# Order of partial products, casts and stores in a hybrid attention, RWKV-7 and feed-forward block

## The chip, the core and the metric

One NeuronCore of a Trainium2 chip runs the whole block. The number is the device time of one execution in microseconds (us). The engines are named as the profile names them: PE (TensorE, matmuls; PEld is its weight loads), DVE (VectorE), ACT (ScalarE), POOL (GpSimd), SP (SyncE, which only issues transfers). Each engine takes its instructions in order from a queue of its own, and waits at the head of the queue for what the next instruction needs.

## The reference

x has 2048 tokens of 1024 channels, all in float32. Cut to what matters here:

```
h  = rms_norm(x, pre_mix_g)
P  = h @ w_in                                   # q, k, v, RWKV inputs, gates
yA = chunk_band_attention(q, k, v, rel_bias)    # 8 heads of 64
yB = rwkv7_time_mix(...)                        # 8 heads of 64
m  = sigmoid(gA) * (yA @ proj_a) + sigmoid(gB) * (yB @ proj_b)   # "branches"
x  = x + rms_norm(m @ w_out, post_mix_g)                         # "output projection"
x  = x + rms_norm(relu(rms_norm(x, pre_ffn_g) @ w_up)**2 @ w_down, post_ffn_g)   # FFN, 4096 wide
```

## The kernel before

Every float32 operand of a matmul is split into a high and a low part (names ending in h and l, or hi and lo): `split` lets ScalarE cast the tile (L78) and VectorE subtract the cast from it (L79). A product is then three matmuls, high by high, low by high, high by low, added in one PSUM bank; a matmul has 512 columns.

The tokens go in four groups of 512 (`G`), one after the other through `phase_rwkv`, `phase_attention` and `phase_merge`; then the FFN runs in two halves of 1024 tokens, each `phase_up` and `phase_down`. In the FFN both weight matrices are cut into 2 by 2 blocks, and seven block products replace eight; the sums of blocks pass through DRAM (xd, wd, td).

**Branches.** `phase_attention` computes the heads in pairs. At its end, while the last pair is still being computed, `load_y` loads and splits the RWKV result (yraw, yh, yl), and `branch` multiplies it by proj_b for eight blocks of 128 channels into ps_p, two banks in turn. A block takes four k tiles with three matmuls each, which `mm3` issues k by k. `phase_merge` then does the same with proj_a. VectorE multiplies each bank by the gate th, which is loaded, at L1097.

**Output projection.** `phase_merge` then multiplies the merged m (mh, ml) by w_out, in two halves of 512 columns (n = 0, 1), weights loaded and split in pairs of k (whi, wlo). Four banks ps_o hold the four tiles of 128 tokens. For each k and each token tile three matmuls are issued in a row. When a half is done, ScalarE squares each bank (sqo, L1136) and VectorE multiplies it by the gain (o, L1137), which frees it. In between come steps of the next group's first norm (`between`: squares L349, scale xn L351, eight transposes pstr L147, casts hh L152 and hl L153) and sums of blocks for the FFN (`beside`, cmb). The next group's first matmul is psd<-hh,whi.

**FFN up.** In tile i of `phase_up` the casts are a1h and a1l of the first weight tile (from i = early = 8 on), s12h, s4h and s3h of block sums; X holds the seven block values that go to DRAM.

**FFN down.** `phase_down` does the block products "1", "6", "7", "5", "4", "3", "2", each in eight steps f. A step loads and splits an activation and a weight tile into one tile fop, two steps ahead. `final(t)` closes an output tile of 128 tokens: square (squ, L1427), gain (L1428), root on POOL (rs), scale and add (L1434), store. The tiles GT + t are complete after product "4", the tiles t after "2"; `advance` runs one step of such a generator. `first_half(2)` loads and splits the next half's activations (bl, bh).

A scheduler orders each engine's queue by the program's order, the buffers that come free and its own estimate of durations; `queue_behind(a, b)` puts a behind b in an engine's order without a wait.

Of the kernel before, what the change touches and what calls it, by code (L numbers as in the profile page):

```python
# [9 lines left out]
F32 = mybir.dt.float32  # L10
# [43 lines left out]
class Block:  # L54
# [1031 lines left out]
    def branch(self, y, br, i):  # L1086

        nc, mp = self.nc, self.bp
        t = mp.tile([P, G], F32, tag="th", bufs=3, name="th")
        nc.sync.dma_start(t, self.gd[br * KB + i])  # L1090
        if i % 2 == 0:
            w = self.a[("proj_a", "proj_b")[br]][:, i * P : (i + 2) * P]
            self.bw = self.wsplit(w.rearrange("(k p) n -> p k n", p=P), "w", NP, 2 * P)
        wh, wl = (x[:, :, i % 2 * P : (i % 2 + 1) * P] for x in self.bw)
        ps = self.pd.tile([P, G], F32, tag="d", name="ps_p")
        self.mm3(ps, [(wh[:, k], wl[:, k], y[0][:, k], y[1][:, k]) for k in range(NP)])
        nc.vector.scalar_tensor_tensor(t, t, 1.0, ps, op0=ALU.add, op1=ALU.mult)  # L1097
        return t

    def phase_merge(self, g, o, op, between, beside):  # L1100

        tc, nc, a = self.tc, self.nc, self.a
        with ExitStack() as ctx:
# [13 lines left out]
            for n in range(2):  # L1117
                ps = [po.tile([P, 512], F32, tag="o", name="ps_o") for _ in range(GT)]
                for k in range(KB):
                    if k % 2 == 0:  # L1120
                        w = a["w_out"][k * P : (k + 2) * P, n * 512 : (n + 1) * 512]
                        wh, wl = self.wsplit(w.rearrange("(j p) n -> p j n", p=P), "w", 2, 512)
                    for t in range(GT):
                        ts = slice(t * P, (t + 1) * P)
                        for j, (l, r) in enumerate(((mh, wh), (mh, wl), (ml, wh))):
                            nc.tensor.matmul(  # L1126
                                ps[t], l[:, k, ts], r[:, k % 2], start=k == 0 and j == 0, stop=k == KB - 1 and j == 2
                            )
                    if n == 0 and k in ((2, 4, 5, 6, 7) if g + 1 < self.NG else (0, 2, 3, 4, 5)):
                        advance(beside, 1)  # L1130
                    if n == 0 and k == 4 or n == 1 and k % 2 == 0:
                        advance(between, 1)
                ns = slice(n * 512, (n + 1) * 512)
                for t in range(GT):
                    sq = op.tile([P, 512], F32, tag="sqo", bufs=2, name="sqo")
                    nc.scalar.activation(sq, ps[t], AF.Square, accum_out=self.ssq[:, g, t, n : n + 1])  # L1136
                    nc.vector.tensor_tensor(o[t][:, ns], ps[t], gp[:, ns], ALU.mult)  # L1137
# [73 lines left out]

    def split_here(self, hi, lo):

        self.nc.scalar.copy(hi, lo.bitcast(F32))
        self.nc.vector.tensor_tensor(lo, lo.bitcast(F32), hi.bitcast(F32), ALU.subtract)

    def first_half(self, g, bp):

        bh, bl = self.b1 = [bp.tile([P, KB, G], F32R, tag="b" + x, name="b" + x) for x in "hl"]
        for k in range(0, KB, 2):  # L1220
            ks = slice(k, k + 2)
            self.nc.sync.dma_start(bl[:, ks].bitcast(F32), self.ht[g][:, ks])
            self.split_here(bh[:, ks], bl[:, ks])
            yield

    def phase_up(self, half, zp, rp, cb, pn, early):
# [6 lines left out]
        with ExitStack() as ctx:  # L1233
# [36 lines left out]
            def parts(src, tag, n):  # L1270
                pool = sp if tag in ("a1", "s12") else late
                hl = [pool.tile([P, n, P], F32R, tag=tag + x, name=tag + x) for x in "hl"]
                self.split(*hl, src)
                return [[x[:, i : i + KH] for x in hl] for i in range(0, n, KH)]

            def hidden(dst, src, x):
# [29 lines left out]
            for i in range(FF // P // 2):  # L1306
# [3 lines left out]
                    nc.sync.dma_start(x, self.xd[0][i // 2][:, i % 2])  # L1310
                (a11, a12), (a21, a22) = ((x[:, lo4], x[:, hi4]) for x in (raw0, raw1))
                if i >= early:
                    A11, A12 = parts(raw0, "a1", KB)
                s12 = up.tile([P, KB, P], F32, tag="s1", name="s12")
                s4 = up.tile([P, KH, P], F32, tag="s4", name="s4")
                nc.vector.tensor_tensor(s12[:, lo4], a21, a22, ALU.add)
# [2 lines left out]

                nc.vector.tensor_tensor(a21, a11, a21, ALU.subtract)  # L1320
                S3, A22 = parts(raw1, "s3", KB)
                nc.vector.tensor_tensor(s4, a12, s12[:, hi4], ALU.subtract)
                (S4,) = parts(s4, "s4", KH)

# [22 lines left out]
    def phase_down(self, half, zp, rp, cb, pn, beside_of):  # L1347
# [4 lines left out]
        with ExitStack() as ctx:  # L1352
# [21 lines left out]
            def operands(s):  # L1374
# [10 lines left out]
                high = self.split(t[:, 2], t[:, 3], wr)  # L1385
                if s == 1:
                    self.queue_behind(self.relu, high)
                return t

            def bank():  # L1390
# [27 lines left out]
            def final(t):  # L1418
# [13 lines left out]
                for n in range(2):  # L1432
# [1 line left out]
                    nc.vector.scalar_tensor_tensor(  # L1434
                        u[t][:, ns], u[t][:, ns], r, x[:, ns], op0=ALU.mult, op1=ALU.add
                    )
                nc.sync.dma_start(self.out[g * G + ts.start : g * G + ts.stop], u[t])
                yield

            NS = len(steps)  # L1440
# [3 lines left out]
            for s, (q, x, w, f) in enumerate(steps):  # L1444
# [12 lines left out]
                for t in range(GT):  # L1457
                    down(ps[t], t, o, f == 0, f == NF // 4 - 1)
                    if f == NF // 4 - 1:
                        gather(q, t, ps[t])  # L1460
                        if q == "4":
                            advance(ends[GT + t])
                        elif q == "3":
                            advance(ends[t], 1)
                        elif q == "2":
                            advance(ends[t])
                if f % 3 == 1 or f == NF // 4 - 1:
                    advance(beside, 1)
            advance(beside)
# [99 lines left out]
```

## Time and profile before

| | |
|---|---|
| median of 3 runs | 3273.53 us (3273.09 to 3274.3) |
| the profiled execution | 3273.41 us, span 3271.7 us |
| PE busy | 3178.6 us, 97%, 18913 matmuls |
| VectorE busy | 2244.4 us, 69% |
| ScalarE busy | 1571.1 us, 48% |
| POOL busy | 592.7 us, 18% |
| transfers | 592.53 MB, 181 GB/s over the span |
| branches and output projection of group 0 | 389.5 to 452.7 us, 452.9 to 501.2 us |
| FFN half 0, up and down | 2019.4 to 2330.5 us, 2330.8 to 2643.2 us |

All times in rows are counted from the start of the span. A row of the timeline gives start, duration, engine, line, operation, the tile written <- the tiles read, shapes and how many instructions of the kind in a row; in brackets stands how long the engine was idle ahead of it and what ended that.

### The profile page before, as it was taken

To read this page: it belongs to the slowest core of one execution; us is meant where nothing else is said; L and a number is where in the kernel's file an instruction comes from. 1 tells how busy PE (TensorE), PEld (TensorE's weight loads), DVE (VectorE), ACT (ScalarE), POOL (GpSimd) and SP (SyncE) were. 2 spreads that over 40 slices of the span, in tenths; PEclk is the share of its full clock that TensorE was granted. 3 is DMA by queue.
4 is the path that set the end of the run, shared out by engine and by line. 5 is a ranking of instruction groups with operands and counts; after the bars stand their busy time and mean duration, and the time that the engine had idled before them with its cause. 6 is when DMAs were issued, how large, how long until landed. Compare 5 with 4: busy or idle time off the path is not lost. (4 is left out here: it accounts for less than half of the span.)

```text
span 3271.7 us, 49957 instructions
## 1 busy us (share of the span) xinstructions
PE 3178.6 (97%) x18913; PEld 2591.9 (79%) x18913; DVE 2244.4 (69%) x3655; ACT 1571.1 (48%) x2511; POOL 592.7 (18%) x1093
## 2 busy tenths in 40 slices
PE   8999999999999999999999999999999999999998
PEld 6777778777878777878777877878888877888887
DVE  7785666776766775776876775777655768775465
ACT  4434634444644434644434754444543444444333
POOL 2221013122112222102222110121211112120000
PEclk9999999999999999999999999999999999999999
DMA  5245373247574237565336557654787875556565
GB/s 167 85 137 175 121 241 119 72 147 245 172 227 133 88 111 246 182 207 164 94 97 225 165 183 256 196 184 149 263 280 251 281 240 185 167 177 228 193 213 180
DMA packets 432282, 592.53 MB, mean 181 GB/s; under 512 B 25301, under 2 KB 295841, under 8 KB 432041
## 3 DMA queue, kind: packets, MB, share of 16 engines
q1 hardware_dynamic: 375080, 413.14, 40.4%
q0 software_dynamic: 47744, 159.42, 13.3%
q10 hardware_dynamic: 9216, 16.78, 1.4%
q8 instruction: 149, 2.44, 0.3%
q14 instruction: 93, 0.75, 0.1%
HBM read 425.37 MB, written 167.01 MB: 181 GB/s over the span
## 5 line engine op out<-in xcount | busy, mean ns | idle before, releaser
L1401 PE MATMUL ps_dn<-fop 128*128 128x512 f32 x2688 | 612.0, 389 | 3.6 <-DVE fop L79 3.6
L1401 PEld LDWEIGHTS ps_dn<-fop 128*128 128x128 f32 x2688 | 503.9, 188 | 109.8 <-DVE fop L79 5.5
L88 PE MATMUL psd<-hh,whi 128*128 128x512 f32 x1344 | 538.9, 403 | 11.9 <-ACT gate L747 6.8
L88 PE MATMUL psd<-hl,whi 128*128 128x512 f32 x1344 | 533.1, 398 | 0.0
L88 PE MATMUL psd<-hh,wlo 128*128 128x512 f32 x1344 | 531.2, 397 | 0.0
L78 ACT CAST whi<-wraw 128x1024 fp32r<-128x1024 f32 x232 | 243.4, 1049 | 425.6 <-PE psd L88 324.2
L79 DVE TENSOR_TENSOR wlo<-wraw,whi 128x1024 fp32r<-128x1024 f32 x232 | 284.6, 1227 | 117.5 <-ACT whi L78 117.2
L88 PEld LDWEIGHTS psd<-hh,whi 128*128 128x128 f32 x1344 | 254.0, 189 | 65.1 <-ACT gate L747 8.9
L88 PEld LDWEIGHTS psd<-hh,wlo 128*128 128x128 f32 x1344 | 252.9, 188 | 50.9 <-issue 0.7
L88 PEld LDWEIGHTS psd<-hl,whi 128*128 128x128 f32 x1344 | 253.2, 188 | 47.2
L79 DVE TENSOR_TENSOR fop<-xraw,fop 128x1024 fp32r<-128x1024 f32 x112 | 137.1, 1224 | 166.8 <-ACT fop L78 165.9
L78 ACT CAST fop<-xraw 128x1024 fp32r<-128x1024 f32 x112 | 117.8, 1052 | 245.2 <-PE ps_dn L1401 163.6
L1283 POOL DMA_DIRECT2D xd<-X x192 | 103.8, 541 | 394.3 <-ACT X L1280 339.5
L79 DVE TENSOR_TENSOR fop<-wdraw,fop 128x1024 fp32r<-128x1024 f32 x112 | 136.8, 1221 | 30.3 <-ACT fop L78 29.9
L78 ACT CAST fop<-wdraw 128x1024 fp32r<-128x1024 f32 x112 | 117.7, 1050 | 46.0 <-DMA wdraw<-in_w_down_dram 29.2
L947 DVE CUSTOM_DVE_ANT_0 sc<-bias,ps_s 128x640 f32<-128x640 f32 (+4 forms) x128 | 93.8, 733 | 57.2 <-PE ps_pt L958 32.1
L952 ACT ACTIVATE sc<-sc,mn 128x640 f32<-128x640 f32 (+4 forms) x128 | 97.7, 764 | 45.5 <-DVE mn L947 44.1
L78 ACT CAST s12h<-s 128x1024 fp32r<-128x1024 f32 x32 | 33.7, 1053 | 164.3 <-PE ps_u L88 164.3
L88 PE MATMUL ps_p<-yh,whi 128*128 128x512 f32 x256 | 101.0, 403 | 7.8 <-DVE th L1097 4.2
L963 DVE TENSOR_TENSOR PTl<-ps_pt,PTh 128x640 fp32r<-128x640 f32 (+4 forms) x128 | 94.3, 737 | 18.4 <-ACT PTh L962 16.9
L1126 PE MATMUL ps_o<-wlo,mh 128*128 128x512 f32 x256 | 100.9, 394 | 3.6 <-DVE wlo L79 3.6
L1126 PE MATMUL ps_o<-whi,mh 128*128 128x512 f32 x256 | 101.5, 396 | 0.8 <-ACT whi L78 0.8
(368 smaller groups left out, 6819.3 us busy)
## 6 DMA issues: line engine op xcount, KB each, us to landing
wraw<-in_w_in_dram SPq DMA_DIRECT2D x168, 512.0 KB
xraw<-xd SPq DMA_DIRECT2D x112, 512.0 KB
xd<-X POOLq DMA_DIRECT2D x192, 256.0 KB, 5.2
wraw<-in_w_up_dram SPq DMA_DIRECT2D x80, 512.0 KB
wdraw<-wd SPq DMA_DIRECT2D x64, 512.0 KB
wdraw<-in_w_down_dram SPq DMA_DIRECT2D x48, 512.0 KB
gd<-gate ACTq DMA_DIRECT2D x64, 256.0 KB
wd<-cmb POOLq DMA_DIRECT2D x64, 256.0 KB, 4.2
```

The lines of the kernel that those rows point to most:

```text
L78: high = self.high = self.nc.scalar.copy(hi, src)
L79: self.low = self.nc.vector.tensor_tensor(lo, src, hi.bitcast(F32), ALU.subtract).ins
L88: mm.append(nc.tensor.matmul(ps, l, r, start=n == 0, stop=n == last).ins)
L947: nc.vector.tensor_tensor_reduce(sc[:, 0:n], bias[:, s0:640], pss[:, c0 : c0 + n], 1.0, 3.0e38, ALU.add, ALU.min, mn,)
L952: nc.scalar.activation(sc[:, 0:n], sc[:, 0:n], AF.Exp, scale=-1.0, bias=mn, accum_out=sm[:, col : col + 1])
L963: nc.vector.tensor_tensor(lv, pst[:, 0:nk], hv.bitcast(F32), ALU.subtract)
L1126: nc.tensor.matmul(ps[t], l[:, k, ts], r[:, k % 2], start=k == 0 and j == 0, stop=k == KB - 1 and j == 2)
L1283: nc.gpsimd.dma_start(self.xd[q][i // 2][:, i % 2], src)
L1401: nc.tensor.matmul(ps, o[:, l, k, sl], o[:, r, k], start=start and n == 0, stop=stop and n == end)
```

## The change

It adds, drops and resizes no operation; the diff moves them.

- `branch` calls `mm3` with `by_part`: high by high for all four k first, then low by high, then high by low.
- The output projection issues each weight pair by parts: eight matmuls whi by mh over the two k and the four token tiles, eight whi by ml, eight wlo by mh. The steps of `between` and `beside` stand behind a whole pair where they stood behind a k.
- In `phase_up`, the first a1h of the main loop (i = early) is queued behind the s3h of the tile before.
- The casts bh of `first_half(2)` are queued behind the second weight cast of `phase_down`.
- The closing tiles GT + t run one at each of the first four steps of product "3" rather than at the end of "4"; in half 0 the output is stored by POOL rather than SP.

```diff
-        self.mm3(ps, [(wh[:, k], wl[:, k], y[0][:, k], y[1][:, k]) for k in range(NP)])
+        self.mm3(ps, [(wh[:, k], wl[:, k], y[0][:, k], y[1][:, k]) for k in range(NP)], True)
...
-                    for t in range(GT):
-                        ts = slice(t * P, (t + 1) * P)
-                        for j, (l, r) in enumerate(((mh, wh), (mh, wl), (ml, wh))):
-                            nc.tensor.matmul(
-                                ps[t], l[:, k, ts], r[:, k % 2], start=k == 0 and j == 0, stop=k == KB - 1 and j == 2
-                            )
+                        for j, (l, r) in enumerate(((mh, wh), (ml, wh), (mh, wl))):
+                            for q in range(2):
+                                for t in range(GT):
+                                    nc.tensor.matmul(
+                                        ps[t], l[:, k + q, t * P : (t + 1) * P], r[:, q],
+                                        start=k + q + j == 0, stop=k + q == KB - 1 and j == 2,
+                                    )
...
+            high = self.split_here(bh[:, ks], bl[:, ks])
+            if g:
+                self.queue_behind(high, self.second)
...
                 if i >= early:
+                    behind = self.cast3
                     A11, A12 = parts(raw0, "a1", KB)
+                    if i == early:
+                        self.queue_behind(self.cast, behind)
...
-                nc.sync.dma_start(self.out[g * G + ts.start : g * G + ts.stop], u[t])
+                queue = nc.sync if half else nc.gpsimd
+                queue.dma_start(self.out[g * G + ts.start : g * G + ts.stop], u[t])
...
-                        if q == "4":
-                            advance(ends[GT + t])
-                        elif q == "3":
+                        if q == "3":
                             advance(ends[t], 1)
                         elif q == "2":
                             advance(ends[t])
+                if q == "3" and f < GT:
+                    advance(ends[GT + f])
```

How the queues change at three places:

TensorE in the attention tail of group 1: ps_s are scores, ps_pt transposes of their softmax, ps_pv its product with the values, ps_p the product with proj_b. Before:

```order
L941 MATMUL ps_s<-KK,QB 128x320
L88 MATMUL ps_p<-yl,whi 128x512
L88 MATMUL ps_p<-yh,wlo 128x512
L88 MATMUL ps_p<-yl,whi 128x512
L88 MATMUL ps_p<-yh,wlo 128x512
L941 MATMUL ps_s<-KK,QA 128x320
L941 MATMUL ps_s<-KK,QB 128x320
L941 MATMUL ps_s<-KK,QA 128x320
L941 MATMUL ps_s<-KK,QB 128x320
L88 MATMUL ps_p<-yh,whi 128x512 x2
L958 MATMUL ps_pt<-ident,sc 128x128 x5
L88 MATMUL ps_p<-yl,whi 128x512
```

and now, from the same instruction (the last of the first block of scores) on:

```order
L941 MATMUL ps_s<-KK,QB 128x320
L941 MATMUL ps_s<-KK,QA 128x320
L941 MATMUL ps_s<-KK,QB 128x320
L941 MATMUL ps_s<-KK,QA 128x320
L941 MATMUL ps_s<-KK,QB 128x320
L88 MATMUL ps_p<-yh,whi 128x512 x2
L958 MATMUL ps_pt<-ident,sc 128x128 x5
L969 MATMUL ps_pv<-PTh_7964,VV 128x256
L1164 MATMUL ps_ht<-ident,o_prev 128x128
```

The four ps_p matmuls with yl and wlo ahead of the second block of ps_s, and the four that begin behind ps_pt, are gone from here; they stand later, behind ps_p's other yh matmuls.

TensorE at the end of group 0's output projection. Before; twelve ps_o matmuls, of which seven are shown, stand between the last pstr and psd, the next group's first:

```order
L1126 MATMUL ps_o<-wlo,mh 128x512
L1126 MATMUL ps_o<-whi,ml 128x512
L147 MATMUL pstr<-ident,xn 128x128 x8
L1126 MATMUL ps_o<-whi,mh 128x512
L1126 MATMUL ps_o<-wlo,mh 128x512
L1126 MATMUL ps_o<-whi,ml 128x512
L1126 MATMUL ps_o<-whi,mh 128x512
L1126 MATMUL ps_o<-wlo,mh 128x512
L1126 MATMUL ps_o<-whi,ml 128x512
L1126 MATMUL ps_o<-whi,mh 128x512
```

and now, up to psd:

```order
L1126 MATMUL ps_o<-wlo,mh 128x512 x8
L147 MATMUL pstr<-ident,xn 128x128 x8
L1126 MATMUL ps_o<-whi,mh 128x512 x8
L1126 MATMUL ps_o<-whi,ml 128x512 x8
L1126 MATMUL ps_o<-wlo,mh 128x512 x8
L147 MATMUL pstr<-ident,xn 128x128 x8
L88 MATMUL psd<-hh,whi 128x512 x2
```

The last transposes pstr stand behind all 24 matmuls of the last pair, right ahead of psd. ScalarE's queue at that place, the difference:

```order
 L152 CAST hh<-pstr 128x4x128 x2
 L78 CAST whi<-wraw 128x1024
+L1137 ACTIVATE sqo,ssqo<-ps_o 128x512 x3
 L152 CAST hh<-pstr 128x4x128 x2
-L1136 ACTIVATE sqo,ssqo<-ps_o 128x512 x4
-L78 CAST whi<-wraw 128x1024 x2
+L1137 ACTIVATE sqo,ssqo<-ps_o 128x512
+L78 CAST whi<-wraw 128x1024
 L361 COPY pr<-psd 128x512
 L364 ACTIVATE lw<-psd,omu 128x512
```

The casts hh of those transposes stand behind three of the four squares sqo.

ScalarE at i = early in the up-projection of half 0. Before:

```order
L78 CAST a1h<-wraw 128x1024
L1279 ACTIVATE X<-X 128x512
L1280 ACTIVATE X<-X 128x512
L78 CAST s4h<-s_21418 128x512
L1279 ACTIVATE X<-X 128x512
L1280 ACTIVATE X<-X 128x512
L78 CAST s3h<-wraw 128x1024
```

and now:

```order
L78 CAST s4h<-s_21531 128x512
L1283 ACTIVATE X<-X 128x512
L1284 ACTIVATE X<-X 128x512
L78 CAST s3h<-wraw 128x1024
L78 CAST a1h<-wraw 128x1024
L1283 ACTIVATE X<-X 128x512
```

The cast a1h of tile 8 stood ahead of the X, s4h and s3h of tile 6; it stands behind the s3h of tile 7.

## Rows read from the trace of the kernel before

**Rows 1.** page, part 1: each engine's busy us, share, instructions

```profile
PE 3178.6 (97%) x18913; PEld 2591.9 (79%) x18913; DVE 2244.4 (69%) x3655; ACT 1571.1 (48%) x2511; POOL 592.7 (18%) x1093
```

**Rows 2.** timeline, FFN: start, us, engine, line, operation, count, [idle before <-releaser]

```profile
2567.38 76.25 PE L1401 MATMUL ps_dn<-fop 128*128 128x512 f32 x335 [1.72 <-DVE fop L79]
```

**Rows 3.** waits of TensorE, whole span: us in total, times, longest

```profile
PE ps_s L941 <- DVE mn L947: 5.8, 5, 1.4
PE ps_p L88 <- DVE th L1097: 4.2, 3, 1.6
PE ps_o L1126 <- DVE wlo L79: 3.6, 5, 1.0
PE ps_u L88 <- ACT s3h L78: 4.1, 2, 2.2
PE ps_u L88 <- DVE s3l L79: 1.0, 2, 0.5
PE ps_dn L1401 <- DVE fop L79: 3.6, 4, 1.7
```

**Rows 4.** timeline, PE and ACT, attention tail of group 1

```profile
899.83 0.41 PE L941 MATMUL ps_s<-KK,QA 128*128 128x320 f32 x1 [1.38 <-DVE mn L947]
906.01 0.73 PE L88 MATMUL ps_p<-yh,whi 128*128 128x512 f32 x2 [1.35 <-ACT yh L78]
905.34 0.62 ACT L78 CAST yh<-yraw 128x512 fp32r<-128x512 f32 x1 [1.55 <-DMA yraw<-yd]
```

**Rows 5.** stretches: us; busy PE, PEld, DVE, ACT, POOL; granted clock; DMA share, GB/s

```profile
895.00:900.00 5.00, 3.62 (x24) 2.95 (x24) 4.72 (x12) 2.77 (x8) 0.00 (x0) 1.00 0.51 160
1992.00:1995.50 3.50, 3.50 (x10) 2.81 (x9) 1.52 (x2) 1.99 (x2) 0.00 (x0) 0.54 1.09 320
```

**Rows 6.** timeline, ACT, DVE, PE, group 0, between output column halves

```profile
474.07 0.60 ACT L1136 ACTIVATE sqo<-ps_o 128x512 f32<-128x512 f32 x1 [2.35 <-PE ps_o L1126]
474.79 2.79 DVE L1137 TENSOR_TENSOR o<-ps_o,g_post 128x512 f32<-128x512 f32 x4 [1.81 <-ACT sqo L1136]
475.91 0.39 PE L1126 MATMUL ps_o<-whi,mh 128*128 128x512 f32 x1
```

**Rows 7.** timeline, PE, ACT, DVE, end of group 0's output projection

```profile
497.63 1.04 PE L147 MATMUL pstr<-ident,xn 128*128 128x128 f32 x8
501.24 0.39 PE L88 MATMUL psd<-hh,whi 128*128 128x512 f32 x1
498.27 1.07 ACT L152 CAST hh<-pstr 128x512 fp32r<-128x512 f32 x2 [2.11 <-PE pstr L147]
499.40 0.60 ACT L1136 ACTIVATE sqo<-ps_o 128x512 f32<-128x512 f32 x1
498.89 1.29 DVE L153 TENSOR_TENSOR hl<-pstr,hh 128x512 fp32r<-128x512 f32 x2 [1.47 <-ACT hh L152]
```

**Rows 8.** timeline, PE and DVE, third weight pair, group 0's output projection

```profile
465.10 0.50 PE L1126 MATMUL ps_o<-wlo,mh 128*128 128x512 f32 x1 [0.95 <-DVE wlo L79]
462.62 1.29 DVE L351 SCALAR_TENSOR_TENSOR xn<-x,rs_r,g_pre 128x1024 f32<-128x1024 f32 x1 [5.23 <-POOL rs_r L127]
```

**Rows 9.** timeline, PE and ACT, FFN half 0, up-projection

```profile
2151.78 0.50 PE L88 MATMUL ps_u<-t3h,s3h 128*128 128x512 f32 x1 [2.21 <-ACT s3h L78]
2146.56 1.05 ACT L78 CAST a1h<-wraw 128x1024 fp32r<-128x1024 f32 x1 [4.29 <-DMA wraw<-in_w_up_dram]
```

**Rows 10.** timeline, PE, ACT, DVE, FFN half 0, down-projection

```profile
2337.69 1.66 PE L1401 MATMUL ps_dn<-fop 128*128 128x512 f32 x6 [1.10 <-DVE fop L79]
2327.78 1.05 ACT L1214 CAST bh<-bl 128x1024 fp32r<-128x1024 f32 x1 [0.46 <-DMA bl<-ht]
2564.78 1.42 DVE L1434 SCALAR_TENSOR_TENSOR u<-u,rs_r,x1r 128x512 f32<-128x512 f32 x2 [0.72 <-POOL rs_r L127]
2566.11 1.22 DVE L79 TENSOR_TENSOR fop<-wdraw,fop 128x1024 fp32r<-128x1024 f32 x1
```

More of the change, by code (lines that the diff above doesn't have):

```diff
@@ L1212, in split_here @@
     def split_here(self, hi, lo):
-        self.nc.scalar.copy(hi, lo.bitcast(F32))
+        high = self.nc.scalar.copy(hi, lo.bitcast(F32))
         self.nc.vector.tensor_tensor(lo, lo.bitcast(F32), hi.bitcast(F32), ALU.subtract)
+        return high.ins
     def first_half(self, g, bp):
@@ L1222, in first_half @@
             self.nc.sync.dma_start(bl[:, ks].bitcast(F32), self.ht[g][:, ks])
-            self.split_here(bh[:, ks], bl[:, ks])
+            high = self.split_here(bh[:, ks], bl[:, ks])
+            if g:
+                self.queue_behind(high, self.second)
             yield
@@ L1272, in parts @@
                 hl = [pool.tile([P, n, P], F32R, tag=tag + x, name=tag + x) for x in "hl"]
-                self.split(*hl, src)
+                self.cast = self.split(*hl, src)
                 return [[x[:, i : i + KH] for x in hl] for i in range(0, n, KH)]
@@ L1321, in phase_up @@
                 S3, A22 = parts(raw1, "s3", KB)
+                self.cast3 = self.cast
                 nc.vector.tensor_tensor(s4, a12, s12[:, hi4], ALU.subtract)
@@ L1387, in operands @@
                     self.queue_behind(self.relu, high)
+                    self.second = high
                 return t
```

## The prediction, made before the changed kernel ran

> **What bounds the kernel.** I read four views in this order. The page's part 1 gives TensorE 3178.6 of 3271.7 us, 97%, while VectorE has 69% and ScalarE 48% [rows 1]: TensorE sets the time, and only its idle stretches can move. The timeline gives the pace when nothing is waited for: 335 matmuls in 76.25 us, one each 0.227 us [rows 2]. A row prints 0.39 us for such a matmul, since its end is modelled, and 0.50 for the first one after a wait [rows 6, 8]; so a wait costs its printed idle time, plus 0.16, plus 0.11, together 0.27 more than printed. The list of TensorE's waits then says for whom it idles [rows 3]: in the places that the change touches these are the scores' minimum mn, the gates' product th, the low cast wlo of w_out, the casts s3h and s3l, and fop. Last comes each place in the timeline of the three engines. The profiled run took 3273.41 us, 0.12 below the median of 3273.53, so I add to 3273.4. The edit adds and removes no matmul, cast or store, so every term is a wait that goes or comes.
>
> **1. proj_b in the attention tail: cost.** load_y's halves arrive while the last pair of heads is still computed, and proj_b's matmuls fill TensorE's pauses there. Multiplied by parts, yh·whi of all four k comes first, so a bank needs the fourth yh before its first yl. The order shows it: eight fillers (two times yl, wlo, yl, wlo) go from between the scores and transposes of group 1, and four more behind the next steps: 12 matmuls, 12 × 0.227 = 2.7 us, now stand after attention work that they filled in before. Do the pauses shrink? TensorE waits 1.38 us for mn at 899.83 and 1.35 for yh at 906.01, whose cast waited 1.55 for the load of yraw [rows 4]. VectorE's chain and the load end where they did, so the eight matmuls ahead of these two waits (1.8 us) are lost surely, the other four perhaps. I take 2.5 between 1.8 and 2.7, in groups 1 to 3: 7.5. In group 0 the order defers 17 matmuls, 3.9 us, but there they stand ahead of transposes that the chain itself waits for, so the chain starts earlier; between 0 and 3.9 I take 1.0. Sum **+8.5**, bounds +5.4 to +12.0.
>
> **2. From n = 0 to n = 1 of the output projection: cost.** There are four ps_o banks, reused by n = 1. Before, each token tile closed its bank with three matmuls of its own, and bank 0's release, the end of the first of four o products at 474.79 + 2.79/4 = 475.49, came 0.42 us ahead of the matmul that needs it at 475.91 [rows 6]. By parts the four banks close in the last four matmuls: bank 0's last one stands 4 ahead of n = 1 and not 10, so the release comes 6 × 0.227 = 1.36 later against it. 1.36 − 0.42 + 0.11 = 1.05 us, four groups: **+4.2**. The later banks ask 0.68 apart, since the scheduler puts three matmuls of one bank together there, and are released 0.70 apart, so nothing more is added. From below it is 0, if TensorE is already late for another reason. From above: ScalarE's order now has one more whi cast ahead of the four squares, 1.05 each if its load lands late, 4.2 more.
>
> **3. The end of a group: cost.** The last transposes (pstr) of the next group's first norm stood twelve matmuls ahead of the end: 497.63 against psd at 501.24 [rows 7]. Now, as the order shows, they stand behind the whole last pair, and ScalarE does three squares before their cast hh. With E the time of psd if nothing were waited for but pstr not yet run: bank 0's last matmul starts at E − 0.9, its square 0.43 later (474.07 against 475.91 − 10 × 0.227 = 473.64 [rows 6]), and three squares, 0.70 apart, end at E + 1.6, the first hh half (1.07 for two [rows 7]) at E + 2.2, the hl half (1.29 for two) behind three o products at E + 3.0. The transposes take 501.24 − 497.63 − 12 × 0.227 = 0.9. So psd waits 1.3 for hh, after two matmuls 0.4 for hl, and 0.2 for two restarts: 1.9 in each of groups 0 to 2, **+5.7**. Bounds +3.3 (hl is hidden) to +7.5.
>
> **4. wlo of w_out: gain.** TensorE waits 3.6 us, five times, for wlo [rows 3]; in group 0 its cast stood behind the scaling xn, 1.29 us that waited for POOL [rows 8]. Low weights are now needed 16 matmuls, 3.6 us, after the high ones, and the longest wait is 1.0: all go. 3.6 + 5 × 0.27 = 4.95. Behind the group 3 waits the granted clock is 0.54 from 1992.0 to 1995.5 us, mostly the lower level of 1.2 GHz; ten matmuls there took 3.5 us and not 2.3, 1.2 lost [rows 5]. A wait for whi stands ahead of it too, which no edit touches, so I count half, 0.6. **−5.6**, bounds −3 to −6.2.
>
> **5. th in the branches** waits 4.2 in three [rows 3]; these are late loads, which stay. TensorE reaches them later: −0.5, bounds 0 to −4.2.
>
> **6. The up-projection: gain.** At i = early ScalarE's first a1h stood 4.29 us at the head of its queue, waiting for a weight load, with X, s4h and s3h behind it, and TensorE waited 2.21 for s3h [rows 9]. In the new order s3h comes first. s3h 4.1 and s3l 1.0, four waits: 5.1 + 4 × 0.27 = 6.2. The clock fell behind the first half's wait; I price that as above, 1.2. **−7.4**, from below −3 if the next cast is late instead. a1h itself is needed only when tile 8 begins.
>
> **7. The down-projection: gain.** bh casts that wait for loads stood ahead of the first fop casts, and TensorE waited 1.10 at 2337.69; at 2567.38, in the block product "3", it waited 1.72, since VectorE had closing tiles (u, 1.42) ahead of the fop cast at 2566.11 [rows 2, 10]. The new order has fop first in both. 1.37 + 1.99 = **−3.4**; the other two fop waits go by loads and stay. Bounds −1.4 to −4.7. The eight stores of half 0 leave SP, where they blocked loads behind u, for POOL, where they wait for the same u with rs steps of later tiles behind them; those are due a product later, so nothing.
>
> **Sum.** 8.5 + 4.2 + 5.7 = 18.4 of cost, 5.6 + 0.5 + 7.4 + 3.4 = 16.9 of gain: +1.5, **3274.9 us**.
>
> **Rivals.**
> *Faster: the out-projection's two new waits do not come.* Both rest on chains reckoned to some tenths; if releases and transposes are covered, 4.2 + 5.7 = 9.9 us fall away: 3265.0. For it: ScalarE and VectorE have slack there. Against: bank 0 had only 0.42 us of reserve [rows 6]. It decides from 8.0 us fewer on.
>
> *Slower: the attention tails starve TensorE until its clock falls.* All deferred matmuls are lost (3.9 + 3 × 2.7 = 12.0) and the clock falls in groups 1 to 3, 3 × 1.2: 15.6 in place of 8.5, 3282.0. For it: the low clock at 1992 came behind such waits. Against: in group 1's tail TensorE is busy 3.62 of 5 us and still granted 1.00 [rows 5], though that is with the fillers. From 13.5 in the tails on it is slower by over 0.2%. Further, if the clock falls at the four bank hand-overs and three group ends too, 7 × 1.2 more: 3290.4. The Trainium skill ("TensorE: Matmul & The Clock Gate", section "A second HAM failure mode: psum-queue depth-cycling") tells of a kernel in which cycling through PSUM banks idled TensorE briefly so often that its clock swung; by that rule the new hand-overs cost the clock as well, which the stretch at 1.00 [rows 5] speaks against.
>
> *Slower: the change does not do in the FFN what it says.* If s3h meets another wait of the same length, 7.4 come back: 3282.3. Against it: s3h's weights are loaded before those a1h waited for.
>
> **How the numbers follow.** About ±0.2%, 6.5 us, is what a measurement of this kernel can tell from no change. My forecast, within that: 0.54. The covered out-projection, and smaller costs in general: 0.22. Starved tails 0.15, further falls of the clock 0.03, the FFN wait 0.06: 0.24 slower. The range, 3264 to 3285, takes in the rivals of both sides except those further falls of the clock.
>
> **What would show it.** In the profile after: no wait of ps_o for wlo and none of ps_u for s3h near a1h (4, 6); waits of ps_o for the o product, once a group and about 0.9 us (2); a wait of psd for hh at each group's first matmul, 1.3 us (3); more idle time of ps_s, ps_pt and ps_p in the four tails, some 8 us in all (1); no low clock at the places of 1992 and 2152, and none in the tails. I am wrong if the tails cost under 4 us or over 13.5, or if the waits of 2 and 3 are missing.

## The result: 0.34% slower, at the upper end of the range

The changed kernel takes 3284.97 us (median of 6 runs, 3281.15 to 3292.91) against 3273.91 for the kernel before (median of 6, 3270.46 to 3275.67). The ratio is 1.0034, with an interval of 1.0023 to 1.0044: slower by more than the measurement is uncertain. I had forecast 3274.9, no difference that can be measured; the time is inside the range, 0.03 us below its upper end. The profiled execution of the changed kernel took 3285.25 us, its span 3283.6, so the two profiles differ by 11.9 us where I had worked out 1.5.

What each engine did in the changed kernel (its page, part 1: busy us, share of the span, instructions):

```profile
PE 3182.9 (97%) x18913; PEld 2596.0 (79%) x18913; DVE 2239.6 (68%) x3655; ACT 1567.9 (48%) x2511; POOL 597.7 (18%) x1101
```

The same 18913 matmuls as in [rows 1], and the same share. So the difference lies in when TensorE works and at what clock. Its waits in the changed kernel, whole span (us in total, times, longest), those that the prediction spoke of and two more of the attention tail (PTh and yh):

```profile
PE ps_s L941 <- DVE mn L947: 10.7, 11, 2.3
PE ps_p L88 <- DVE th L1097: 9.3, 9, 3.3
PE ps_pv L969 <- ACT PTh L962: 4.3, 8, 0.8
PE ps_p L88 <- ACT yh L78: 2.8, 2, 1.5
PE ps_o L1126 <- DVE o L1138: 2.8, 4, 0.8
PE psd L88 <- ACT hh L152: 2.6, 3, 0.9
PE ps_dn L1410 <- DVE fop L79: 1.2, 3, 0.8
PE ps_dn L1410 <- ACT fop L78: 0.6, 1, 0.6
PE psd L88 <- DVE hl L153: 0.5, 3, 0.2
```

Against [rows 3]: mn has risen from 5.8 to 10.7, th from 4.2 in three waits to 9.3 in nine. The waits for o, hh and hl are new and were forecast. The rows for wlo, s3h and s3l are gone, and fop has halved.

In the term by term account below, steps 1, 6 and 7 are lengths from the two timelines, from the start of one named matmul to that of another. In steps 2 to 5 a wait counts as the prediction counted it, its printed idle time plus 0.27 us.

| step of the prediction | forecast | the two profiles |
|---|---|---|
| 1. attention tails | +8.5 | +12.1 |
| 2. hand-over n = 0 to n = 1, o | +4.2 | +3.9 |
| 3. end of a group, hh and hl | +5.7 | +4.7 |
| 4. wlo | −5.6 | −5.0 |
| 5. th | −0.5 | +6.7 |
| 6, 7. FFN | −10.8 | −10.9 |
| sum | +1.5 | +11.5 (measured 11.9) |

The sum closes to 0.4 us, but in part because its rows make up for each other. Between named matmuls throughout, with the matmuls deferred out of the tails put to step 1, the stretches from the tails to the output projections (step 5) give +5.6, and the output projections (steps 2 to 4) give +1.8 where the rows add to +3.6, since in group 3 a wait of 0.83 for whi and the low clock at 1992 went as well. Of the FFN's 10.9, 0.9 are four ps_u matmuls that now stand in group 3's output projection. The up-projections are 8.0 us shorter without them and the down-projections 2.0. The RWKV stretches, for which the prediction had no term, are 2.4 longer.

For step 1, the time from the first ps_p to the last ps_pv of each group, with the number of ps_p matmuls that stand inside it:

| tail, us | before | after | e2 | e9 |
|---|---|---|---|---|
| group 0 | 23.14 (32) | 22.38 (15) | 22.27 (15) | 20.75 (27) |
| group 1 | 33.30 (47) | 33.18 (35) | 35.94 (35) | 33.17 (45) |
| group 2 | 33.32 (47) | 33.16 (35) | 33.21 (35) | 33.86 (45) |
| group 3 | 32.25 (47) | 33.35 (35) | 34.41 (35) | 32.68 (45) |

(e2 and e9 are experiments below; e9's count has added matmuls in it.) A tail that is as long as before although 17 or 12 matmuls were taken from it has lost them: they are still to be done behind it, at 0.227 us each [rows 2]. So group 0 cost −0.76 + 3.86 = 3.1, groups 1 and 2 cost 2.6 each, group 3 1.10 + 2.72 = 3.8: 12.1.

**The tail in the trace.** TensorE in the tail of group 1, changed kernel (timeline, columns as in [rows 4]):

```profile
905.76 0.41 PE L941 MATMUL ps_s<-KK,QA 128*128 128x320 f32 x1 [2.33 <-DVE mn L947]
908.56 0.39 PE L969 MATMUL ps_pv<-PTh,VV 128*128 128x256 f32 x1 [0.78 <-ACT PTh L962]
911.89 0.72 PE L88 MATMUL ps_p<-yh,whi 128*128 128x512 f32 x2 [1.37 <-ACT yh L78]
```

The first row answers to 899.83 in [rows 4]: 2.33 of idle time where 1.38 were. The four fillers that stood ahead of it took 0.9, and the wait is longer by 0.95. The wait for yh, 1.35 in [rows 4], is the same; the fillers taken from ahead of it show as waits for PTh instead, 4.3 us in eight over the span where the kernel before has 0.9 in two.

**The two new waits.** Group 0 between the column halves, TensorE, ScalarE and VectorE, then the group's end, TensorE and ScalarE (timeline of the changed kernel):

```profile
479.47 0.60 ACT L1137 ACTIVATE sqo<-ps_o 128x512 f32<-128x512 f32 x1
480.19 2.48 DVE L1138 TENSOR_TENSOR o<-ps_o,g_post 128x512 f32<-128x512 f32 x4 [4.20 <-ACT sqo L1137]
480.94 0.73 PE L1126 MATMUL ps_o<-whi,mh 128*128 128x512 f32 x2 [0.82 <-DVE o L1138]
...
505.56 1.03 PE L147 MATMUL pstr<-ident,xn 128*128 128x128 f32 x8
506.81 1.08 ACT L152 CAST hh<-pstr 128x512 fp32r<-128x512 f32 x2
507.45 0.73 PE L88 MATMUL psd<-hh,whi 128*128 128x512 f32 x2 [0.85 <-ACT hh L152]
508.34 0.50 PE L88 MATMUL psd<-hl,whi 128*128 128x512 f32 x1 [0.15 <-DVE hl L153]
```

Against [rows 6] the first o product starts 0.75 ahead of the matmul that needs its bank, where it had started 1.12 ahead; the matmul waits. Against [rows 7] the last transposes stand directly ahead of psd, and their cast hh behind three squares.

**th.** VectorE, then TensorE, then the issues of th loads on SP, in group 1 of the changed kernel:

```profile
927.16 0.69 DVE L1097 SCALAR_TENSOR_TENSOR th<-th,ps_p 128x512 f32<-128x512 f32 x1 [0.43 <-PE ps_p L88]
933.78 0.69 DVE L1097 SCALAR_TENSOR_TENSOR th<-th,ps_p 128x512 f32<-128x512 f32 x1 [1.26 <-PE ps_p L88]
942.32 0.69 DVE L1097 SCALAR_TENSOR_TENSOR th<-th,ps_p 128x512 f32<-128x512 f32 x1 [2.39 <-DMA th<-gd]
947.93 0.69 DVE L1097 SCALAR_TENSOR_TENSOR th<-th,ps_p 128x512 f32<-128x512 f32 x1 [3.79 <-DMA th<-gd]
948.77 1.16 PE L88 MATMUL ps_p<-yh,whi 128*128 128x512 f32 x4 [1.41 <-DVE th L1097]
932.42 0.32 SPq L1090 DMA_DIRECT2D th<-gd  x1
939.50 0.32 SPq L1090 DMA_DIRECT2D th<-gd  x1
```

and the same product and loads in the kernel before:

```profile
918.17 0.67 DVE L1097 SCALAR_TENSOR_TENSOR th<-th,ps_p 128x512 f32<-128x512 f32 x1
921.53 0.69 DVE L1097 SCALAR_TENSOR_TENSOR th<-th,ps_p 128x512 f32<-128x512 f32 x1
923.07 0.32 SPq L1090 DMA_DIRECT2D th<-gd  x1
927.05 0.32 SPq L1090 DMA_DIRECT2D th<-gd  x1
```

Count from the group's first ps_p, 894.15 before and 900.05 after. Before, the second and third bank were multiplied 24.0 and 27.4 us on; after, 27.1 and 33.7. th has three buffers, each free for the next load when the product written into it has been stored to DRAM (md<-th). The loads shown went out 28.9 and 32.9 us on before, 32.4 and 39.5 after. From there on TensorE needs a th every 2.7 us, and the loads, issued 3 to 7 us later, are what it waits for.

**The clock.** Stretches of the changed kernel (us; busy PE, PEld, DVE, ACT, POOL; granted clock; DMA share, GB/s): two tails, the bank hand-over, a group's end, and the branches of group 3:

```profile
396.00:402.80 6.80, 6.08 (x21) 4.48 (x21) 2.85 (x11) 3.27 (x10) 0.00 (x0) 0.53 0.43 154
1928.80:1932.30 3.50, 3.12 (x11) 2.41 (x11) 1.93 (x5) 1.90 (x5) 0.00 (x0) 0.53 0.18 51
479.00:485.00 6.00, 5.17 (x23) 3.93 (x23) 3.62 (x5) 2.90 (x10) 0.00 (x0) 1.00 0.26 73
505.00:511.00 6.00, 5.00 (x26) 3.70 (x25) 4.81 (x7) 3.40 (x11) 3.49 (x13) 1.00 0.49 189
1987.00:1990.50 3.50, 3.11 (x8) 2.48 (x9) 3.42 (x6) 0.62 (x1) 0.00 (x0) 0.51 0.76 216
```

In the tails of groups 0 and 3 the granted clock is 0.53, mostly the lower level of 1.2 GHz. Those are the two tails in the table that cost more than 2.6. In group 0 the kernel before was not free of it either, for half as long:

```profile
394.40:397.80 3.40, 2.94 (x10) 1.53 (x8) 1.21 (x4) 1.42 (x5) 0.55 (x1) 0.50 0.66 240
```

At the hand-over and at the group's end the changed kernel keeps 1.00; behind the longest wait for th it has 0.51.

### The profile page after: what moved, and what is told of

Read it like the earlier page. It is cut to its first block, busy times and chain, and to the rows that moved or that the text cites. A ratio compares the mean times of both kernels' runs of the same rounds, so it can differ in the third digit from the quotient of the medians.

```text
span 3283.6 us, 49974 instructions
## 1 busy us (share of the span) xinstructions
PE 3182.9 (97%) x18913; PEld 2596.0 (79%) x18913; DVE 2239.6 (68%) x3655; ACT 1567.9 (48%) x2511; POOL 597.7 (18%) x1101
## 5 line engine op out<-in xcount | busy, mean ns | idle before, releaser
L78 ACT CAST s12h<-s 128x1024 fp32r<-128x1024 f32 x32 | 33.7, 1052 | 162.8 <-PE ps_u L88 162.8
L962 ACT CAST PTh<-ps_pt 128x640 fp32r<-128x640 f32 (+4 forms) x128 | 79.8, 623 | 42.4 <-PE ps_pt L958 41.1
L958 PE MATMUL ps_pt<-ident,sc 128*128 128x128 f32 x560 | 84.1, 277 | 5.0 <-DVE PTl L963 4.4
L88 PE MATMUL ps_p<-yh,whi 128*128 128x512 f32 x256 | 76.7, 411 | 12.3 <-DVE th L1097 9.3
```

Source lines behind the costliest of these rows:

```text
L78: high = self.high = self.nc.scalar.copy(hi, src)
L88: mm.append(nc.tensor.matmul(ps, l, r, start=n == 0, stop=n == last).ins)
L958: nc.tensor.transpose(pst[:, j], sc[:, j * P : (j + 1) * P], self.ident)
L962: nc.scalar.copy(hv, pst[:, 0:nk])
```

## The experiments

Each ratio is against runs of the kernel before on the same chip. e1 to e4 ran beside one set of its runs (median 3270.11 us), e5 to e8 beside another (3270.81), e9 to e11 beside a third (3272.55).

### The change in parts: e1, e2, e3

e1, the FFN's edits alone (first lines of each; the rest as in the diff above):

```diff
+                if i == early:
+                    self.queue_behind(self.cast, behind)
...
+                queue = nc.sync if half else nc.gpsimd
...
+                if q == "3" and f < GT:
+                    advance(ends[GT + f])
```

> The kernel before with the FFN's edits alone (casts a1h and bh queued anew, closing tiles at product "3", half 0's stores on POOL). If the parts add up as the two traces lie side by side (up and down stages of the changed kernel 6.4, 2.0 and 2.5 us shorter than before), this is 10.9 us faster than before, 3263. The rival, that the FFN gained only because it began later relative to its loads, gives under 5 us: 3269 or more.

Measured: 3259.55 us, ratio 0.9967 (0.9954 to 0.998), −10.6 us. Steps 6 and 7 together hold alone as they hold in the whole; the interval, −15.0 to −6.5, does not part them.

e2, the branches by parts alone:

```diff
-        self.mm3(ps, [... for k in range(NP)])
+        self.mm3(ps, [... for k in range(NP)], True)
```

> The kernel before with the branches by parts alone. Theory: the attention tails lose 2.6 to 2.8 us in each of groups 1 to 3 and about 1 less in group 0, 7 us; the waits of ps_p for th grow by 4 to 5 us beyond that; with one to three more falls of the clock at 1.2 us this is 12 to 15 us slower than before, 3286 to 3289. The rival, that only the tails cost and th grew through the output projection's edit, gives 7 to 8 us: 3281 to 3282.

Measured: 3291.73 us (3283.75 to 3294.49), ratio 1.0067 (1.005 to 1.0084), +21.6 us. That is more than either theory gave, and more than the whole change costs. Its waits:

```profile
PE ps_s L941 <- DVE mn L947: 10.4, 10, 2.3
PE ps_p L88 <- DVE th L1097: 6.9, 9, 1.6
```

and, from the view of the gate product's line L1097, how long VectorE sat idle ahead of it until a load landed (us, times):

```profile
  DMA th<-gd: 27.1, 19
```

The profile is that of its fastest run, 3283.75 us. In it the tails cost 15.8 by the table above and th 2.7 + 6 × 0.27 = 4.3; 5.8 us of that are offset ahead of the tails, in the RWKV stretches that e2 does not touch and that differ by some us from run to run, and some 2 at the waits of the output projection. (Between named matmuls th's part is 1.9, and the sum then comes within half a us of the 10.3 by which the two profiles differ.) The waits for mn are those of the changed kernel, those for th 2.4 us less. What is new is the clock, low in three of the four tails. Stretches of e2 in the tails of groups 0, 1, 1 and 3, columns as above:

```profile
391.70:398.50 6.80, 5.46 (x18) 4.15 (x18) 3.30 (x11) 3.46 (x10) 0.56 (x1) 0.50 0.46 168
896.80:900.30 3.50, 3.21 (x11) 2.65 (x11) 1.93 (x6) 1.72 (x5) 0.56 (x1) 0.51 0.25 69
910.50:914.00 3.50, 3.35 (x12) 2.96 (x12) 2.17 (x4) 1.61 (x4) 0.00 (x0) 0.51 0.00 0
1917.40:1924.20 6.80, 6.02 (x23) 5.00 (x23) 3.36 (x7) 3.69 (x8) 0.00 (x0) 0.50 0.15 41
```

In the third of them e2 does 12 matmuls at 0.51. Groups 1 and 2 run the same instructions; as far behind its first ps_p as that stretch, group 2 has a clock of 1.00:

```profile
1423.05:1426.55 3.50, 3.50 (x26) 3.10 (x24) 1.68 (x5) 2.17 (x4) 0.00 (x0) 1.00 0.00 0
```

In this profile the clock fell in group 1's tail and not in group 2's, and group 1's took 35.94 us, group 2's 33.21: 2.7 us for two falls. Over the four runs the mean granted clock was 0.992 to 0.995 (0.9930 on the mean, before 0.9962), and the run at 0.995 was 7 to 11 us faster than the three at 0.992 and 0.993. One thousandth of the mean clock is 3.3 us of TensorE's work in a span of 3272, so 0.0032 would be 10.5 us, an upper bound, since TensorE is not short of time everywhere.

e3, the output projection by parts alone:

```diff
-                        for j, (l, r) in enumerate(((mh, wh), (mh, wl), (ml, wh))):
+                        for j, (l, r) in enumerate(((mh, wh), (ml, wh), (mh, wl))):
+                            for q in range(2):
+                                for t in range(GT):
```

> The kernel before with the output projection by parts alone. Theory: o's release costs 3.9 us (four times 0.7 and the restart), the next group's first matmuls 5.2 (three times 1.75), the waits for wlo give back 5.0 and the low clock in group 3 up to 1.2: 3 to 4 us slower, 3277 to 3278, with ps_p's waits for th as before, about 4 us. The rival, that this edit also makes th late, shows th waits of 8 us or more and 3281.

Measured: 3271.95 us, ratio 1.0011 (1.0002 to 1.002), +1.8 us. Steps 2 to 4 together, +4.3, lie in the interval of 0.7 to 6.5. Its waits are those of the changed kernel, o in four and hh in three, and wlo is gone. The three ratios multiply to 0.9967 × 1.0067 × 1.0011 = 1.0045; the whole has 1.0034.

### Where in the branches: e4, e5

Two causes were open for th's longer waits: the order of SP's loads, which the change moves too, and the late start of the ring of buffers in the tail. e4, by parts in proj_a alone, outside the tail, with SP's order as in the changed kernel:

```diff
+        self.mm3(ps, [... for k in range(NP)], br == 0)
```

> The kernel before with proj_a alone by parts; proj_b, which runs in the attention tail, stays k by k. SP's order of loads in the proj_a stage (weights of w_out ahead of mb and th) is that of the whole change. Theory R: th is late because the first banks close later in the tail and the ring of three th buffers starts late; then nothing is late here: th waits about 4 us as before, 3273 to 3275. Rival S: th is late because SP issues w_out's weights first; then th waits grow to 7 us or more here, 3277 or more.

Measured: 3268.85 us, ratio 0.9998 (0.9987 to 1.001). th waits 5.0 in six. Neither SP's order nor by parts in blocks that follow each other costs anything that can be measured (the interval is −4.3 to +3.3 us).

e5, the changed kernel with only the first two blocks of proj_b, those in the tail, k by k:

```diff
-        self.mm3(ps, [... for k in range(NP)], True)
+        self.mm3(ps, [... for k in range(NP)], br == 0 or i > 1)
```

> The changed kernel with one thing undone: proj_b's first two blocks, the ones in the attention tail, go k by k again; all other blocks stay by parts. Theory: those two blocks carry the whole cost of the branches (the lost fillers, the late ring of th loads, the falls of the clock), so the rest adds up to the FFN's gain (10.5) and the output projection's cost (1.8): 8 to 9 us faster than before, with no low clock in the tails of groups 1 to 3 and th waits of 4 to 5 us. Rival: by parts costs also in the later blocks; then this is no faster than before.

Measured: 3265.9 us, ratio 0.9984 (0.9975 to 0.9994): 4.9 us faster than the kernel before, where the whole change is slower. Its waits:

```profile
PE ps_s L941 <- DVE mn L947: 5.8, 5, 1.4
PE ps_p L88 <- DVE th L1097: 4.2, 4, 2.0
```

mn and th are back at their values of [rows 3], the four tails take 23.37, 33.20, 33.29 and 32.20 us, and the mean clock of its ten runs is 0.9969 (before 0.9958). So the tails, th and the clock all come from two blocks out of sixteen in each group. From the account above, 11.5 − 12.1 − 6.7 = −7.3 would remain; −4.9 agrees with it within its interval of −8.2 to −2.0. The −8 to −9 that I expected lies at the edge.

### th or the clock: e6, e9

e6, e2 with a fourth buffer for th (and one fewer for mb, for room):

```diff
-        t = mp.tile([P, G], F32, tag="th", bufs=3, name="th")
+        t = mp.tile([P, G], F32, tag="th", bufs=4, name="th")
```

> The kernel before with the branches by parts (as e2_branch_parts) and four buffers for th in place of three; mb has two in place of three to make room. Theory: th is late because three buffers come free only when the tail's late banks are read; with four the waits of ps_p for th fall from 6.9 us to 4 or less, and the time is 3 to 5 us under e2_branch_parts, still 15 us or more over before, since the lost fillers and the low clock stay. Rival: the loads themselves are slow; then the th waits stay at 6 to 7 us and so does the time.

Measured: 3286.69 us, ratio 1.0042 (1.0027 to 1.0057), +15.9 us where e2 had +21.6, each against its own runs of the kernel before. The two intervals, 8.8 to 18.6 and 16.4 to 27.5, overlap, so the times alone do not show a gain; the waits do. VectorE's idle time ahead of L1097 until a load landed, the one wait of TensorE for th that is left, with the VectorE row that it goes back to, and the stretch behind it:

```profile
  DMA th<-gd: 0.8, 2
```

```profile
1973.95 1.23 DVE L1215 TENSOR_TENSOR bl<-bl,bh 128x1024 fp32r<-128x1024 f32 x1 [3.23 <-ACT bh L1214]
1976.43 1.59 PE L88 MATMUL ps_p<-yh,whi 128*128 128x512 f32 x4 [2.52 <-DVE th L1097]
```

```profile
1977.00:1980.50 3.50, 3.50 (x10) 2.71 (x9) 3.00 (x5) 1.31 (x2) 0.00 (x0) 0.51 0.92 307
```

VectorE's waits for th loads fall from 27.1 us to 0.8 (the kernel before has 19.0): the loads were late because of the ring. The one wait left has another cause. In group 3 the gate product stands in VectorE's queue behind bl of the FFN's first activations, which waits 3.23 for its cast bh, and that for its load; the clock falls behind it. The changed kernel has the same at 1987.39 (3.27 of its 9.3), the kernel before a shorter one at 1963.04 (1.50 of 4.2). So of th's growth of 5.1 us of idle time 3.3 go with the ring and 1.8 with bl. The mean clock stayed at 0.992 to 0.995 in the four runs, so the ring's waits are not what lowers it.

e9 tests the clock itself: e2 with two matmuls by zero weights behind each high by high of the first two blocks, 64 in all, 14.5 us of TensorE's time.

```diff
             n += 1
+            if zero is not None and n <= len(terms):
+                for _ in range(2):
+                    nc.tensor.matmul(ps, zero, r, start=False, stop=False)
```

> The kernel before with the branches by parts (as e2_branch_parts), and in proj_b's first two blocks two extra matmuls with an all-zero weight tile after each high-by-high one. They add nothing to the result, and stand in the tail's pauses where the low-part matmuls stood before; the deferred matmuls stay deferred. Theory: of e2_branch_parts' 21.6 us some 10 are the clock, which falls because TensorE is emptier in the tails; with the fillers the mean granted clock of the runs comes back from 0.992 to 0.995 or more, and the time falls by 3 to 8 us, to 3284 to 3288, although 64 matmuls (14.5 us of TensorE, most of it in pauses) are added. Rival: the clock falls for another reason, or costs little; then the added matmuls only cost, 3293 to 3297, at a clock of 0.992 to 0.993.

Measured: 3291.01 us, ratio 1.006 (1.004 to 1.008), +18.5 us; mean clock of four runs 0.9952, of the kernel before on that chip also 0.9952. The stretches at the times that were low in e2, tails of groups 0 and 3, columns as above:

```profile
391.70:398.50 6.80, 5.67 (x33) 4.44 (x34) 4.15 (x13) 4.86 (x14) 0.13 (x1) 1.00 0.46 157
1917.40:1924.20 6.80, 4.04 (x19) 2.50 (x18) 5.24 (x13) 4.17 (x11) 0.00 (x0) 1.00 0.28 81
```

The clock is back in three tails of four. In group 2, where it had not fallen in e2, it now does:

```profile
1411.80:1415.20 3.40, 2.77 (x10) 1.65 (x8) 1.65 (x4) 0.86 (x3) 0.56 (x1) 0.50 0.45 151
```

With ten to twelve more matmuls in each, the tails of groups 0, 1 and 3 are 1.5, 2.8 and 1.7 us shorter than in e2, and that of group 2 is 0.7 longer: −5.4 us in all. But the tails hold only 42 matmuls more than e2's where 64 were added; 22 of them, 5.0 us, are work behind the tails, and th waits 8.4. The gain was spent, so the time as a whole, which did not come down to what I expected, does not give the clock's price. What e2's tails show is 1.4 us for each of the two falls in group 1, against the 1.2 that I had taken.

A cleaner price lies in group 0. Its tail holds the same 32 ps_p matmuls in all kernels but the changed one, e2, e6 and e9, and none of them waits for th inside it. It takes 22.17 us in e11, where the clock stayed up, 23.10 to 23.37 in the kernel before, e1, e3, e4 and e5, where it was low for 3.4 us, and 24.43 to 24.62 in e7, e8 and e10, where it was low for 6.8 us. The tail of e11, then the low stretch of e10:

```profile
389.85:412.02 22.17, 18.27 (x99) 13.41 (x99) 16.40 (x40) 14.10 (x37) 1.64 (x3) 1.00 0.32 109
393.30:400.10 6.80, 6.34 (x22) 4.79 (x21) 3.25 (x10) 3.47 (x10) 0.23 (x1) 0.50 0.46 157
```

By the means the first 3.4 us at the lower level cost 1.0 us there and the second 1.4, and in group 0 the clock falls with the fillers too. In groups 1 to 3 the count speaks for the fillers: with them the clock stayed at 1.00 in all 27 tails of those nine kernels, without them (the changed kernel, e2, e6) it fell in five of nine, and with zero weights in one of three.

### The FFN's part, and versions that are faster: e10, e7, e8, e11

e10, the cast a1h behind s3h alone:

```diff
+                    behind = self.cast3
                     A11, A12 = parts(raw0, "a1", KB)
+                    if i == early:
+                        self.queue_behind(self.cast, behind)
```

> The kernel before with one FFN edit alone: the first a1h of the main loop queued behind the s3h of the tile before. Theory: that is the 7.4 us reckoned for it (6.2 of waits for s3h and s3l, 1.2 of clock), the larger part of the FFN edits' 10.5: 3263 against 3270. Rival: the closing tiles and the casts of bh carry half or more of the gain; then this gives 5 us or less.

Measured: 3262.11 us, ratio 0.9964 (0.9953 to 0.9976), −10.4 us. TensorE has no wait for s3h or s3l, and the waits of product "3" stay:

```profile
PE ps_dn L1405 <- DVE fop L79: 3.3, 4, 1.3
```

One cast behind another gives at least as much as I had said of it, −7.4, and by the medians all that e1 gives; the interval, −15 to −8, leaves room for some of step 7. In its profile the two up-projections are 4.5 and 3.4 us shorter than before, and the down-projections are not shorter.

e7, the output projection by parts, but with the last pair of each half token tile by token tile, and the next group's norm steps after the first eight matmuls of a pair:

```diff
+                        tiles = [(j, q, t) for j in range(3) for q in range(2) for t in range(GT)]
+                        if k == KB - 2:
+                            tiles.sort(key=lambda x: x[2])
+                        for m, (j, q, t) in enumerate(tiles):
...
+                            if m == 7 and (n == 0 and k == 4 or n == 1):
+                                advance(between, 1)
```

> The kernel before with the output projection by parts, but with the last weight pair of each half token tile by token tile (whi by mh, whi by ml, wlo by mh of one bank, then the next), so that the banks close 1.36 us apart, and with the norm's steps after the first eight matmuls of a pair. Theory: the two new waits of e3_out_parts (for o 3.9, for hh and hl 5.2) are made by the banks closing together and by the transposes standing last; both go, and wlo's gain stays: 9 us under e3_out_parts, some 5 to 7 under before, 3263 to 3265. Rival: the waits come from the casts' order on ScalarE; then psd's wait for hh stays at 2 us or more.

Measured: 3265.41 us, ratio 0.9982 (0.9972 to 0.9992), −5.4 us where e3 had +1.8. No wait for hh, hl or wlo is left, and one for o, for which the list of e3 and then that of e7 read:

```profile
PE ps_o L1126 <- DVE o L1138: 5.3, 4, 2.4
```

```profile
PE ps_o L1128 <- DVE o L1140: 1.5, 1, 1.5
```

So steps 2 and 3 were right in their cause too: with the banks closing apart and the transposes ahead of the last matmuls, both waits go and wlo's gain remains.

e8, e1 with e7's output projection, the branches k by k:

```diff
+                        if k == KB - 2:
+                            tiles.sort(key=lambda x: x[2])
...
+                    if i == early:
+                        self.queue_behind(self.cast, behind)
```

> The FFN's edits of the change, the output projection as in e7_out_spaced, the branches k by k as before. If the parts add up: 10.5 and 5 to 7 us faster than before, ratio 0.995, 3253 to 3255; faster than both kernels. Rival: the FFN's gain is taken up by the FFN's own loads when it begins earlier; then no better than e1_ffn_only, 3259 to 3260.

Measured: 3259.16 us, ratio 0.9962 (0.9949 to 0.9975), −11.7 us, faster than both kernels. The two gains would add to −16.0; the interval, −16.7 to −8.2, holds that as well as e1's −10.6 alone, so how far they add is open.

e11, e8 with four th buffers:

```diff
+        t = mp.tile([P, G], F32, tag="th", bufs=4, name="th")
```

> e8_ffn_out_spaced with four buffers for th and two for mb. Theory: ps_p's remaining waits for th (3.4 us in e8_ffn_out_spaced) go, as in e6_th4: 2 to 3 us under it, ratio 0.9955. Rival: two buffers for mb make its loads late instead; no faster than e8_ffn_out_spaced.

Measured: 3258.2 us, ratio 0.9958 (0.9943 to 0.9972), −14.4 us: the fastest of all, though not by more than its interval. One wait for th is left, 2.4 us.

## Why the prediction was wrong, point by point

**Steps 2, 3, 4 and 6 were right**, each within 1.0 us of its term, and e3, e7 and e10 show their causes. Step 7 gave 2.0 us and not 3.4: the waits at 2337.69 and 2567.38 went, but the other waits of the first product are 1.56 us where the kernel before has 0.62, as they are 1.50 in e10 without step 7's edits. No run tests step 7 alone. The first o product of [rows 6] had a reserve of 0.42, and six matmuls fewer ahead of n = 1 turned it into a wait, as worked out. The waits for hh came as 0.9 and not 1.3, those for hl as 0.2 and not 0.4, with two restarts 1.6 a group against 1.9.

**Step 5 failed, by 7.2 us of the 10.4 missed** (by 6.1 if it is taken between named matmuls). I wrote of the th waits that "these are late loads, which stay", and that TensorE would reach them later: −0.5, with bounds of 0 and −4.2. No bound lay on the side of a cost. The loads do not stay: a th load is issued when the product of an earlier bank has been stored, and step 1 itself, by putting off the low weights, puts off the closing of the first banks. The third bank of group 1 was multiplied 6.3 us later against the group's start. I had followed the twelve deferred matmuls to TensorE and not to the buffers that their banks release. e6 shows the ring as the cause of most of it; the rest, the longer wait behind bl in group 3, was no part of the prediction either. Why bl's load took longer there (issued at 1976.69, its cast started at 1983.83) is not settled.

**Step 1 was right in kind and mis-sized by 3.6 us.** In groups 1 and 2, where the clock did not fall, the cost is 2.6 for the 2.5 that I took: nearly all twelve fillers are lost. What was wrong is group 0, 3.1 for 1.0, where I let the chain start earlier by most of what it lost, and group 3, 3.8 for 2.5. In both the granted clock was at the lower level 3.4 us longer than before. At the 1.2 us that this costs on the mean in group 0's tail (under e9), it accounts for some 2.4 of the 3.6. The sum had no term for that; it stood as the slower rival alone, with a chance of 0.15 and 15.6 us of tails. In the changed kernel's profile that rival came half true (12.1). In e2 it came true in full, 15.8, with falls in groups 0, 1 and 3. What I set against it, the stretch at 1.00 in [rows 5], was with the fillers, as I said there and did not price. My last line, no low clock in the tails, is refuted by the rows at 396.00 and 1928.80. Group 0's tail was low before the change already, at 394.40, a stretch that is not among my rows.

**The further rival**, that the clock falls at hand-overs and group ends too, did not come in the changed kernel: 1.00 in both stretches shown, and no low stretch at the other hand-overs and group ends. The Trainium skill ("TensorE: Matmul & The Clock Gate", section "A second HAM failure mode: psum-queue depth-cycling") has short idle times between groups of matmuls swing the clock. The waits of 0.8 us for a PSUM bank, with dense matmuls around them, did not do it here. In e3, where group 3's hand-over waited 2.45 us, the clock fell behind it (0.51 from 1995.1 to 1998.5); behind a wait of 3.0 at the same place in e4 it did not. The tails are nearer to what that section describes: pauses of 0.2 to 2.3 us in quick succession, and there it fell, in some groups and not in others.

**What stays open.** The clock's part of the changed kernel's median: between 60 and 3250 us the changed kernel's profile is at the lower level for 27.3 us and that of the kernel before for 17.1, which at 1.2 us for 3.4 is an estimated 3.6 us; the mean clocks of e2's and e6's runs suggest more, and e9 could not price it. Nor is it settled which tails fall in a given run.

## What to carry to other kernels

When matmuls are put off, ask what their bank's closing releases, and follow that to the load queue: a ring of three buffers passed a late start on to the loads behind it here. Matmuls that fill the pauses of a latency chain are worth their own time and, in some executions, the clock as well, so a change of order may be sound in a dense stretch and cost in the tail ahead of it; try it there apart (two blocks of sixteen held the whole loss). For a wait that is said to stay, write down the bound on the side of a loss too.

## What was not expected of the hardware

In groups 1 to 3 it hung on a dozen matmuls of 0.227 us whether the clock can fall in a tail: with them it did in none of 27, without them in five of nine (0.51 in group 1 of e2, 910.5 to 914.0). Matmuls by zero weights in their place brought it back in most tails (from 0.50 to 1.00 at 1917.4 to 1924.2 us, group 3), not in all. Under the same instructions it fell in one group and not in the next, and group 0's tail took 22.2, 23.1 or 24.4 us by how long it was low, so one profile does not show what the median pays. In e2 the runs between 0.995 and 0.992 of mean clock lie 10.7 us apart.
